# A trunk kernel's hand-overs between matmul stages: products, PSUM copies and tiles in another order

## The chip, the cores and the metric

The kernel runs on one core of one Trainium2 chip. The metric is the device time of one execution in microseconds; before the change it is 2490.99 us (median of 3 runs, 2490.53 to 2492.29).

## The reference

The input x is 256 tokens by 4096. All tensors are float32. One layer is computed, and a final RMSNorm:

```python
h = rms_norm(x, norm_gains)
z = h @ w_in             # gq gk gv gg gdec sq sk sv sg ga gb, 19472 columns
o_a = gla_mix(gq, gk, gv, log_a)             # chunked gated linear attention, 8 heads
y_a = (rms_norm(o_a, gain) * silu(gg)) @ w_gla_out         # 2048 x 4096
o_b = swa_sink_mix(sq, sk, sv, sinks)        # sliding window, 32 query heads
y_b = (o_b * silu(sg)) @ w_swa_out           # 2048 x 4096
merged = sigmoid(ga + b0) * y_a + sigmoid(gb + b1) * y_b
x = x + merged @ w_out                       # 4096 x 4096
out = rms_norm(x, final_norm_gain)
```

## The kernel before

A float32 product is made of three matmuls: each operand is split into a rounded half (`hi`, type float32r) and the rest (`lo`), and hi·hi, hi·lo and lo·hi are summed in one PSUM bank (lines 162 to 164 and 234 to 236). ScalarE (ACT) casts `hi` from a loaded weight chunk of 128x1024, VectorE (DVE) subtracts to get `lo`; `halves` does this for every chunk. SP issues the weight loads.

TensorE goes through the stages in this order: the GLA blocks (`gq gk gv gg`, by `gemm`, 192 matmuls for a block of 512 columns), `ya` (`spilled`: four pairs of blocks; the sums are copied to `ya_d` and sent to DRAM), the sliding-window blocks (`sk sv sq sg`), `yb` (as `ya`), eight pairs `ga0 gb0 ga1 ... gb3` of the merge gates, whose results are multiplied with the reloaded y and summed in `m`, and four pairs `o0` to `o3` of the last product with `mT`, the transposed m.

`pair` computes two blocks of 512 columns for both row tiles, 8 contractions j (`ya`, `yb`) or 16 (`ga`, `gb`, `o`). A plain j takes eight products, each of three matmuls, into banks 2, 3, 4 and 8. For the j in the table `SEVEN` it takes seven (a Strassen-like scheme, one product fewer) that also use banks 1, 5, 6 and 7; for this DVE forms three sums of weight chunks (`t`, `u`, `s`, lines 214 to 216), and `combine` forms the matching sums of the left factor once for a whole stage (`xca`, `xcb`, `xch`, `xcm`). The first pair of a stage takes all eight products in every j, since its `combine` is not made yet. Before the change the table begins with j = 0.

At the end of a pair `outputs` copies bank 1 with ACT (line 253) and adds the other seven on DVE (line 247). All eight banks are then in use, and the next pair's first products go to banks that must be emptied first.

At the end of a GLA or window stage the gated result is transposed by TensorE (`transpose_split`, line 288) into `oaT` or `obT`, with a cast on ACT (line 278) and a subtraction on DVE (line 279); after `gb3` sixteen such steps make `mT` from `m`. At the start `first_inputs` makes hT, the scaled input, chunk by chunk during `gq`, squares the input on ACT (line 129) and adds the squares on GpSimd (line 130). At the end the kernel adds x, squares, takes the sum and scales (lines 655 to 669).

A scheduler of the framework puts the instructions in order. Each engine takes its own in that order, one by one. `tc.high_priority` (400 for `gemm`, 120 for `pair`) lets loads, casts and subtractions slip ahead. DMAs that ACT issues (y, bias, spills) stand in ACT's queue and wait there for what they send.

## Time and profile before

| | |
|---|---|
| median of 3 runs | 2490.99 us |
| the profiled execution | 2495.09 us |
| its span, first to last instruction | 2493.4 us |
| TensorE busy | 2437.6 us, 98% |
| VectorE, ScalarE busy | 1724.6 us, 1225.4 us |
| HBM | 476.61 MB read, 12.58 MB written |

The profiled execution is 4.1 us longer than the median, and its span leaves 1.7 us of it outside. The granted TensorE clock (PEclk) is 1.00 at the full 2.4 GHz and 0.50 at 1.2 GHz; a window's number is the mean. A matmul's listed length overlaps the next one's; the pace is the distance between starts.

### The profile page before, as it was taken

Reading aid. Unit: us, or ns where it says so; the run is one execution under the profiler, and the core shown is the slowest. Engines: PE = TensorE matmul, PEld = TensorE weight load, DVE = VectorE, ACT = ScalarE, POOL = GpSimd, SP = SyncE. Lnnn points to the kernel's source line nnn. Section 1 sums busy time; section 2 is a strip of 40 time slices with the busy share of each in tenths; the row PEclk is TensorE's granted clock in tenths of the full one; section 3 lists DMA queues with packets and bytes.
Section 4 is the critical chain, followed back from the end, with each engine's and each line's share of the span. In section 5 each row is a group of like instructions: output and inputs, shape, how many; then the busy total and the mean of one; then the engine's idle time right before and its main releaser. Section 6 shows DMA issues by size and latency. Waiting matters only on the chain.

```text
span 2493.4 us, 29365 instructions
## 1 busy us (share of the span) xinstructions
PE 2437.6 (98%) x10986; PEld 1999.0 (80%) x10986; DVE 1724.6 (69%) x1929; ACT 1225.4 (49%) x1479; POOL 42.5 (2%) x52
## 2 busy tenths in 40 slices
...
GB/s 250 157 169 192 170 176 194 170 170 204 191 223 183 192 179 160 152 186 152 161 178 193 218 245 185 213 227 228 216 216 227 216 227 216 202 186 216 225 221 191
DMA packets 139024, 491.14 MB, mean 197 GB/s; under 512 B 15840, under 2 KB 16224, under 8 KB 138880
## 3 DMA queue, kind: packets, MB, share of 16 engines
...
HBM read 476.61 MB, written 12.58 MB: 196 GB/s over the span
## 4 chain that ended last, share of the span: by engine, by line
PE 89%; DVE 5%; issue 2%; DMA 2%; ACT 1%; POOL 0%; SPq 0%; ACTq 0%; POOLq 0%; DVEq 0%
PE ga_q L234 5%; PE ga_q L236 4%; PE ga_q L235 4%; PE gb_q L236 4%; PE gb_q L234 4%; PE gb_q L235 4%; PE o_q L236 4%; PE o_q L235 4%; PE o_q L234 4%; PE sg_a L163 2%; PE sg_a L162 2%; PE sq_a L164 2%; PE sq_a L163 2%; PE sq_a L162 2%; PE sg_a L164 2%; PE gg_a L164 2%
## 5 line engine op out<-in xcount | busy, mean ns | idle before, releaser
L214 DVE TENSOR_TENSOR gb_t<-gb_r,gb_s 128x1024 f32<-128x1024 f32 x24 | 29.3, 1221 | 11.0 <-DMA gb_s<-in_wgate_dram 11.0
L103 POOL TENSOR_TENSOR st<-st,mhalf 128x1 f32<-128x1 f32 x2 | 1.1, 553 | 1700.4 <-DVE st L102 1700.4
L565 ACT ACTIVATE s<-s,mx 128x128 f32<-128x128 f32 x64 | 28.4, 445 | 0.0
L214 DVE TENSOR_TENSOR o_t<-o_r,o_s 128x1024 f32<-128x1024 f32 x18 | 22.0, 1221 | 9.1 <-DMA o_s<-in_wout_dram 9.1
L130 POOL TENSOR_TENSOR ssq<-ssq,sq 128x512 f32<-128x512 f32 x15 | 26.4, 1757 | 25.3 <-ACT sq L129 24.7
L214 DVE TENSOR_TENSOR ga_t<-ga_r,ga_s 128x1024 f32<-128x1024 f32 x18 | 22.0, 1221 | 4.9 <-DMA ga_s<-in_wgate_dram 4.7
L121 DVE SCALAR_TENSOR_TENSOR hT<-xsb,gin_sb,hT 128x256 fp32r<-128x256 f32 x32 | 21.9, 733 | 4.9 <-ACT hT L120 4.9
L550 DVE SCALAR_TENSOR_TENSOR s<-s,mask 128x384 f32<-128x384 f32 x32 | 16.0, 552 | 6.0 <-PE s L549 6.0
L143 ACT CAST sg_16h<-sg_r 128x1024 fp32r<-128x1024 f32 x4 | 4.2, 1056 | 28.0 <-PE sg_a L164 28.0
L214 DVE TENSOR_TENSOR ya_t<-ya_r,ya_s 128x1024 f32<-128x1024 f32 x9 | 11.0, 1222 | 8.6 <-DMA ya_s<-in_wgla_dram 8.6
L214 DVE TENSOR_TENSOR yb_t<-yb_r,yb_s 128x1024 f32<-128x1024 f32 x9 | 11.0, 1222 | 8.4 <-DMA yb_s<-in_wswa_dram 8.4
L657 ACT ACTIVATE xt<-x 128x512 f32<-128x512 f32 x16 | 10.1, 630 | 13.7 <-DVE x L247 13.7
L216 DVE TENSOR_TENSOR gb_s<-gb_u,gb_s 128x512 f32<-128x512 f32 x24 | 16.5, 688 | 0.3
L215 DVE TENSOR_TENSOR gb_u<-gb_t,gb_r 128x512 f32<-128x512 f32 x24 | 16.5, 688 | 0.3
L473 DVE COPY oraw<-op 128x512 f32<-128x512 f32 x8 | 5.5, 692 | 15.6 <-PE op L472 15.6
L582 DVE COPY pT<-pt 128x384 f32<-128x384 f32 x16 | 8.9, 554 | 9.3 <-PE pt L579 9.3
L464 POOL TENSOR_SCALAR_AFFINE_SELECT ats<-ats 128x128 f32<-128x128 f32 x16 | 8.0, 523 | 415.4 <-DVE ats L462 415.4
L476 ACT ACTIVATE jk<-oraw 128x256 f32<-128x256 f32 x16 | 6.7, 418 | 16.9 <-DVE oraw L473 16.6
L579 PEld LDWEIGHTS pt<-ident,s 128*128 128x128 f32 x96 | 11.4, 145 | 4.4 <-ACT s L565 3.9
L120 ACT ACTIVATE hT<-xsb,gin_sb 128x256 fp32r<-128x256 f32 x32 | 14.1, 499 | 1.8 <-DMA xsb<-in_xT_dram 1.2
L579 PE MATMUL pt<-ident,s 128*128 128x128 f32 x96 | 14.9, 278 | 0.0
L288 PE MATMUL m_t<-ident,m 128*128 128x128 f32 x64 | 10.2, 302 | 3.7 <-DVE mT L279 3.7
...
## 6 DMA issues: line engine op xcount, KB each, us to landing
...
```

Of the source, the lines that this page charges most:

```text
L121: nc.vector.scalar_tensor_tensor(hT[:, kt, 1, :], xsb[:, kt, :], g, hT[:, kt, 0, :].bitcast(F32), ALU.mult, ALU.subtract)
L130: nc.gpsimd.tensor_tensor(ssq, ssq, sq, ALU.add)
L162: nc.tensor.matmul(acc[t], lh, hi[:, i, :], start=kt == 0, stop=False)
L163: nc.tensor.matmul(acc[t], lh, lo[:, i, :], start=False, stop=False)
L164: nc.tensor.matmul(acc[t], ll, hi[:, i, :], start=False, stop=kt == nkt - 1)
L214: nc.vector.tensor_tensor(ts, r1, r2[:, 0:1, :].broadcast_to([P, 2, NB]), ALU.add)
L215: nc.vector.tensor_tensor(t2[:, 0, :], ts[:, 1, :], r1[:, 0, :], ALU.add)
L234: nc.tensor.matmul(q[i], lh, hi[:, c, :], start=done[i] == 1, stop=False)
L235: nc.tensor.matmul(q[i], lh, lo[:, c, :], start=False, stop=False)
L236: nc.tensor.matmul(q[i], ll, hi[:, c, :], start=False, stop=done[i] == total[i])
L565: nc.scalar.activation(s4[:, k, cs], s4[:, k, cs], AF.Exp, bias=mx[:, k, t : t + 1], accum_out=sm[:, k, t : t + 1],)
L579: nc.tensor.transpose(tp[:, m * P : (m + 1) * P], s4[:, k, m * P : (m + 1) * P], ident)
```

## The change

The diff is below; in words:

- **Products.** `SEVEN` becomes (1, 4, 6, 9, 11, 13) for 16 contractions and (1, 3, 5) for 8, so every pair begins with eight products into banks 2, 4, 3 and 8. The first pairs of `ya`, `yb` and the gates now use seven products from contraction 4 (`ya0`, `yb0`: j = 5) or 8 (`ga0`: j = 9, 11, 13) on; `first_pair` spreads `combine` over their first contractions. `o0` keeps eight throughout.
- **End of a pair.** The last contraction's eight products are sorted by bank (2, 4, 3, 8), so that the sums end one after the other. ACT copies these four and bank 1; DVE makes eight additions, five of them with a PSUM operand.
- **Last gate pair.** `gb3` and `o3` keep the additions of before; sums of `gb3` are followed at once by transposes (`merged`), the rest of the gate comes behind, and the last four transposes and the `combine` of `mT` stand inside `o0`.
- **Tiles.** `oraw`, `ss`, `gt`, `gng_sb`, `on` and `sg` move to pools of their own (`glo`, `slo`), and the staging tiles of mixed stages are laid out in a fixed order (`mixed_staging`), so the first loads and casts of `ya` and `yb` reuse other memory than before.
- **Squares.** Written in the loop of `gk` instead of that of `gq`.
- **End of the kernel.** x is loaded in one piece per pair and added in `outputs`; seven of eight partial sums of squares are reduced early; the last gain is applied with the final scaling; the output goes in six pieces per row tile instead of four.

```diff
-SEVEN = {16: (0, 3, 5, 8, 10, 13), 8: (0, 2, 5)}
+SEVEN = {16: (1, 4, 6, 9, 11, 13), 8: (1, 3, 5)}
...
+        def squares(k0, n):
             xr = xsb[:, k0 : k0 + n, :]
-            if k0 < KW:
-                nc.scalar.activation(ssq[:, k0 : k0 + n, :], xr, AF.Square)
+            if k0 == 0:
+                nc.scalar.activation(ssq, xr, AF.Square)
                 return
             sq = gp.tile([P, KW, S], F32, tag="sq", name=f"sq{k0}", bufs=2)
             nc.scalar.activation(sq, xr, AF.Square)
             nc.gpsimd.tensor_tensor(ssq, ssq, sq, ALU.add)
 
-        return before
+        return before, squares
...
+    def mixed_staging():
+
+        cur["n"], cur["r"] = STM, 6
+        for tag, n, dt, bufs in (("hi", 2, F32R, STM), ("raw", 2, F32, 6), ("t2", 1, F32, 1), ("t13", 2, F32, 1), ("lo", 2, F32R, STM)):
+            cur["hl"].tile([P, n, NB], dt, tag=tag, name=f"first_{tag}", bufs=bufs)
+
+    def combine(lhs, xc, js, name, at=None):
 
 
         for c, j in enumerate(js):
+            if at is not None and at != c:
+                continue
...
-        sev = SEVEN[npr] if xc is not None else ()
+    def pair(name, lhs, w, npr, xc=None, before=None, last=False, since=0):
+
+        sev = [j for j in SEVEN[npr] if j >= since] if xc is not None else ()
...
+            if not last and j == npr - 1:
+                work.sort(key=lambda x: (2, 4, 3, 8).index(x[0]))
             if last and j == npr - 1:
-                work.sort(key=lambda x: x[0] in (4, 8))
+                work.sort(key=lambda x: {4: 1, 8: 2}.get(x[0], 0))
...
-    def outputs(q, d, name, pool):
-
+    def outputs(q, d, name, pool, extra=None, late=None):
+
+
+        quarters = ((0, 0, 2), (1, 0, 4), (0, 1, 3), (1, 1, 8))
         if 1 in q:
             v = pool.tile([P, NB], F32, tag="yr", name=f"{name}_v", bufs=2)
+        if 1 in q and late is None:
+            for t, i, b in quarters:
+                nc.scalar.copy(d[t][i], q[b])
+            nc.scalar.copy(v, q[1])
+            add(d[0][0], q[1], d[0][0])
+            add(v, q[6], v)
+            add(d[0][1], q[5], d[0][1])
+            add(d[1][1], q[5], d[1][1])
+            add(d[0][1], d[0][1], v, ALU.subtract)
+            add(v, q[7], v)
+            add(d[1][0], d[1][0], v)
+            add(d[1][1], d[1][1], v, ALU.subtract)
+        elif 1 in q:
             nc.scalar.copy(d[0][0], q[1])
             add(v, q[6], d[0][0])
             add(d[0][1], q[5], v, ALU.subtract)
             add(d[1][0], q[7], v)
             add(d[1][1], q[5], d[1][0], ALU.subtract)
-        for t, i, b in ((0, 0, 2), (0, 1, 3), (1, 0, 4), (1, 1, 8)):
-            if 1 in q:
+        for do in (late or ())[:1]:
+            do()
+        for t, i, b in quarters:
+            if 1 not in q:
+                if extra is not None:
+                    add(d[t][i], q[b], extra[t][i])
+                else:
+                    nc.scalar.copy(d[t][i], q[b])
+                continue
+            if extra is not None:
+                add(d[t][i], d[t][i], extra[t][i])
+            if late is not None:
                 add(d[t][i], q[b], d[t][i])
-            else:
-                nc.scalar.copy(d[t][i], q[b])
+        for do in (late or ())[1:]:
+            do()
+
+    def first_pair(lhs, xc, npr, name, order, since, n):
+
+        if n > 0:
+            return {}
+
+        def before(j):
+            if 1 <= j <= len(order):
+                combine(lhs, xc, SEVEN[npr], name, at=order[j - 1])
+
+        return {"before": before, "since": since}
 
     def spilled(name, lhs, w, dst, xc, pool):
 
         for n in range(NP2):
-            q = pair(f"{name}{n}", lhs, w[n], OKT // 2, xc=None if n == 0 else xc)
+            q = pair(f"{name}{n}", lhs, w[n], OKT // 2, xc=xc, **first_pair(lhs, xc, OKT // 2, name, (2, 0, 1), 4, n))
...
+    with phase("hl0") as cur["hl"], phase("gla") as gp, phase("glo") as glo:
         cur["n"], cur["r"] = STG, 4
         ssq = gp.tile([P, KW, S], F32, name="ssq")
-        q0 = zblock("gq", 0, before=first_inputs(gp, ssq), chunks=RAMP)
-        k0 = zblock("gk", 0)
+        load, squares = first_inputs(gp, ssq)
+        q0 = zblock("gq", 0, before=load, chunks=RAMP)
+        k0 = zblock("gk", 0, before=squares)
...
-                gt = gp.tile([P, NT, 2 * DV], F32, tag="gt", name=f"gt{pi}")
+                gt = glo.tile([P, NT, 2 * DV], F32, tag="gt", name=f"gt{pi}")
...
-        cur["n"], cur["r"] = STM, 6
+        mixed_staging()
...
+    mTs = []
+
+    def merged(j0, j1):
+
+        if j0 == 0:
+            mTs.append(big.tile([P, KT, 2, S], F32R, tag="hT", name="mT"))
+        for j in range(j0, j1):
+            transpose_split(mTs[0], 2 * j, m[:, :, 2 * j * P : 2 * (j + 1) * P], 2, f"m{j}")
+
     for n in range(NP2):
         for w, (kind, y_d) in enumerate((("ga", ya_d), ("gb", yb_d))):
             cs = [slice((2 * n + i) * NB, (2 * n + i + 1) * NB) for i in range(2)]
             bt = ep.tile([P, 2, NB], F32, tag="bt", name=f"bt{w}{n}")
             nc.scalar.dma_start(bt, bgates[w, 2 * n * NB : 2 * (n + 1) * NB].partition_broadcast(P).rearrange("p (i c) -> p i c", i=2))
-            q = pair(f"{kind}{n}", hT, wgate[w * NP2 + n], KT // 2, xc=None if n + w == 0 else xch)
-            if n + w == 0:
-                combine(hT, xch, SEVEN[KT // 2], "h")
+            q = pair(
+                f"{kind}{n}", hT, wgate[w * NP2 + n], KT // 2, xc=xch,
+                **first_pair(hT, xch, KT // 2, "h", (3, 4, 5, 0, 1, 2), 8, n + w),
+            )
             d = ep.tile([P, NT, 2, NB], F32, tag="ev", name=f"{kind}_d{n}")
-            outputs(q, [[d[:, t, i, :] for i in range(2)] for t in range(NT)], f"{kind}{n}", ep)
+            mt = [lambda: merged(0, 2), lambda: merged(2, 3 * KT // 8)] if w == 1 and n == NP2 - 1 else None
...
-    st = ep.tile([P, NT, NBLK + 1], F32, tag="ev", name="st")
-    for j in range(KT // 2):
-        transpose_split(mT, 2 * j, m[:, :, 2 * j * P : 2 * (j + 1) * P], 2, f"m{j}")
+    st = const.tile([P, KT], F32, tag="kt", name="st")[:, : NT * (NBLK + 1)].rearrange("p (t n) -> p t n", t=NT)
     x2 = big.tile([P, NT, DM], F32, tag="oT", name="x2")
+    sf = [st[:, t, NBLK:] for t in range(NT)]
+    sums = lambda j: (
+        combine(mT, xcm, SEVEN[KT // 2], "m", at=j - 9) if j >= 9
+        else transpose_split(mT, 2 * (j + 10), m[:, :, 2 * (j + 10) * P : 2 * (j + 11) * P], 2, f"m{j + 10}") if 2 <= j < 6
+        else None
+    )
...
+        q = pair(f"o{n}", mT, wout[n], KT // 2, xc=None if n == 0 else xcm, last=last, before=sums if n == 0 else None)
...
-        outputs(q, [[x2[:, t, cs[i]] for i in range(2)] for t in range(NT)], f"o{n}", ep)
         gf = ep.tile([P, 2, NB], F32, tag="bt", name=f"gf{n}")
         nc.scalar.dma_start(gf, gfin[2 * n * NB : 2 * (n + 1) * NB].partition_broadcast(P).rearrange("p (i c) -> p i c", i=2))
+        xt = ep.tile([P, NT, 2, NB], F32, tag="ev", name=f"xt{n}")
+        nc.scalar.dma_start(xt, x[:, 2 * n * NB : 2 * (n + 1) * NB].rearrange("(t p) (i c) -> p t i c", p=P, i=2))
+        outputs(
+            q, [[x2[:, t, cs[i]] for i in range(2)] for t in range(NT)], f"o{n}", ep,
+            extra=[[xt[:, t, i, :] for i in range(2)] for t in range(NT)], late=[] if last else None,
+        )
         for t in range(NT):
             for i in range(2):
                 xq = x2[:, t, cs[i]]
-                xt = ep.tile([P, NB], F32, tag="yr", name=f"xt{n}{t}{i}", bufs=2)
-                nc.scalar.dma_start(xt, x[t * P : (t + 1) * P, cs[i]])
-                add(xq, xq, xt)
-                nc.scalar.activation(xt, xq, AF.Square, accum_out=st[:, t, 2 * n + i : 2 * n + i + 1])
-                add(xq, xq, gf[:, i, :], ALU.mult)
+                nc.scalar.activation(xt[:, t, i, :], xq, AF.Square, accum_out=st[:, t, 2 * n + i : 2 * n + i + 1])
+                if not last or i == 0:
+                    add(xq, xq, gf[:, i, :], ALU.mult)
+                if last and i == 0:
+
+                    nc.vector.tensor_reduce(sf[t], st[:, t, : NBLK - 1], AX.X, ALU.add)
+                    nc.vector.tensor_scalar(sf[t], sf[t], 1.0 / DM, EPS, ALU.mult, ALU.add)
     for t in range(NT):
-        sf = st[:, t, NBLK:]
-        nc.vector.tensor_reduce(sf, st[:, t, :NBLK], AX.X, ALU.add)
-        rms_scale(sf, sf, DM)
-        for c in range(4):
-            os = slice(c * 1024, (c + 1) * 1024)
-            if c % 2 == 0:
-                nc.vector.tensor_scalar(x2[:, t, os], x2[:, t, os], sf, None, ALU.mult)
+        nc.vector.tensor_scalar(sf[t], st[:, t, NBLK - 1 : NBLK], 1.0 / DM, sf[t], ALU.mult, ALU.add)
+        nc.gpsimd.tensor_tensor(sf[t], sf[t], mhalf[:, 0:1], ALU.pow)
+        at = 0
+        for c, w in enumerate((512, 512, 1024, 1024, 512, 512)):
+            os = slice(at, at + w)
+            at += w
+            if at == DM:
+                nc.vector.scalar_tensor_tensor(x2[:, t, os], x2[:, t, os], sf[t], gf[:, 1, :], ALU.mult, ALU.mult)
+            elif c % 2 == 0:
+                nc.vector.tensor_scalar(x2[:, t, os], x2[:, t, os], sf[t], None, ALU.mult)
             else:
-                nc.scalar.activation(x2[:, t, os], x2[:, t, os], AF.Copy, scale=sf)
+                nc.scalar.activation(x2[:, t, os], x2[:, t, os], AF.Copy, scale=sf[t])
             nc.sync.dma_start(out[t * P : (t + 1) * P, os], x2[:, t, os])
```

Three places show how the instruction order moves. The first is ACT between the pairs `ga1` and `gb1`: `ga_d1` is the tile of ga1's results, `q2` to `q8` are banks, `r`, `s`, `t`, `u` are weight chunks and their sums, and `h` marks a cast. Before:

```order
L143 CAST ga1_s15h_12597<-ga1_s15_12591 128x1024
L143 CAST gb1_t0h_12675<-gb1_t0_12670 128x1024
L143 CAST gb1_u0h_12679<-gb1_u0_12671 128x512
L626 DMA yga100_12636<-ya_d_63 128x512
L143 CAST gb1_r0h_12683<-gb1_r0_12666 128x1024
L626 DMA yga101_12641<-ya_d_63 128x512
L143 CAST gb1_s0h_12687<-gb1_s0_12668 128x1024
L143 CAST gb1_r1h_12716<-gb1_r1_12712 128x1024
L143 CAST gb1_s1h_12720<-gb1_s1_12714 128x1024
```

After:

```order
L145 CAST gb1_r0h_12811<-gb1_r0_12807 128x1024
L145 CAST gb1_s0h_12815<-gb1_s0_12809 128x1024
L145 CAST gb1_t1h_12852<-gb1_t1_12847 128x1024
L269 COPY ga_d1_12762<-ga1_q2_12122 128x512
L269 COPY ga_d1_12762<-ga1_q4_12124 128x512
L686 ACTIVATE ga_d1_12762<-ga_d1_12762 128x512
L269 COPY ga_d1_12762<-ga1_q3_12123 128x512
L145 CAST gb1_u1h_12856<-gb1_u1_12848 128x512
L684 DMA yga101_12782<-ya_d_63 128x512
L145 CAST gb1_r1h_12860<-gb1_r1_12843 128x1024
L269 COPY ga_d1_12762<-ga1_q8_12125 128x512
L145 CAST gb1_s1h_12864<-gb1_s1_12845 128x1024
```

The four copies and a sigmoid (line 686) now stand between the casts for the first two contractions of `gb1`; the reloads of y come behind.

The second is ACT between `ya3`, the last pair of `ya`, and `sk0`, the first window block; the DMA rows send the sums to DRAM. Before:

```order
L143 CAST ya3_r7h_5546<-ya3_r7_5542 128x1024
L253 COPY ya_d3_5578<-ya3_q1_5252 128x512
L143 CAST ya3_s7h_5550<-ya3_s7_5544 128x1024
L271 DMA ya_d_63<-ya_d3_5578 128x1024 x2
L143 CAST sk0_0h_5616<-sk0_r0_5614 128x1024
```

After:

```order
L270 COPY ya3_v_5619<-ya3_q1_5292 128x512
L145 CAST ya3_s7h_5590<-ya3_s7_5584 128x1024
L269 COPY ya_d3_5618<-ya3_q2_5296 128x512
L269 COPY ya_d3_5618<-ya3_q4_5298 128x512
L269 COPY ya_d3_5618<-ya3_q3_5297 128x512
L269 COPY ya_d3_5618<-ya3_q8_5299 128x512
L319 DMA ya_d_63<-ya_d3_5618 128x1024 x2
L145 CAST sk0_0h_5663<-sk0_r0_5661 128x1024
```

The four copies, and the two DMAs that wait for them and for DVE's additions, stand ahead of the first cast of `sk0`.

The third is DVE between `gb3` and `o0`: `gb_d3` holds gb3's results, `m` the merged rows, the rows of `mT` are the lower halves of transposed pieces `m0`, `m1` and so on, and those with `o0` prepare weight chunks. Before:

```order
L247 TENSOR_TENSOR gb_d3_16018<-gb3_q4_15380,gb_d3_16018 128x512
L247 TENSOR_TENSOR gb_d3_16018<-gb3_q8_15381,gb_d3_16018 128x512
L627 SCALAR_TENSOR_TENSOR gb_d3_16018<-gb_d3_16018,rstd_82,bt13_15372 128x512 x3
L247 TENSOR_TENSOR gb_d3_16018<-gb_d3_16018,ygb300_16029 128x512
L247 TENSOR_TENSOR gb_d3_16018<-gb_d3_16018,ygb301_16035 128x512
L247 TENSOR_TENSOR m_10636<-m_10636,gb_d3_16018 128x512 x2
L627 SCALAR_TENSOR_TENSOR gb_d3_16018<-gb_d3_16018,rstd_82,bt13_15372 128x512
L279 TENSOR_TENSOR mT_16053<-m0_t0_16056,mT_16053 128x2x256
L247 TENSOR_TENSOR gb_d3_16018<-gb_d3_16018,ygb310_16041 128x512
L247 TENSOR_TENSOR gb_d3_16018<-gb_d3_16018,ygb311_16047 128x512
L247 TENSOR_TENSOR m_10636<-m_10636,gb_d3_16018 128x512 x2
L279 TENSOR_TENSOR mT_16053<-m1_t0_16063,mT_16053 128x2x256
```

After:

```order
L259 TENSOR_TENSOR gb_d3_16175<-gb3_q3_15536,gb_d3_16175 128x512
L685 SCALAR_TENSOR_TENSOR gb_d3_16175<-gb_d3_16175,rstd_82,bt13_15529 128x512
L259 TENSOR_TENSOR gb_d3_16175<-gb3_q8_15538,gb_d3_16175 128x512
L146 TENSOR_TENSOR o0_s1l_16347<-o0_s1_16340,o0_s1h_16346 128x1024
L325 TENSOR_TENSOR mT_16182<-m0_t0_16183,mT_16182 128x2x256
L325 TENSOR_TENSOR mT_16182<-m1_t0_16190,mT_16182 128x2x256
L325 TENSOR_TENSOR mT_16182<-m2_t0_16201,mT_16182 128x2x256
L325 TENSOR_TENSOR mT_16182<-m3_t0_16208,mT_16182 128x2x256
L146 TENSOR_TENSOR o0_r2l_16386<-o0_r2_16381,o0_r2h_16385 128x1024
L325 TENSOR_TENSOR mT_16182<-m4_t0_16215,mT_16182 128x2x256
```

The lower halves of `m0` and the following pieces now come right behind gb3's last sum; the multiplications with y and the additions into `m` come after `m11`.

## Rows read from the trace of the kernel before

**Rows 1.** The page, part 1: busy us of each engine.

```profile
PE 2437.6 (98%) x10986; PEld 1999.0 (80%) x10986; DVE 1724.6 (69%) x1929; ACT 1225.4 (49%) x1479; POOL 42.5 (2%) x52
```

**Rows 2.** Windows of stages: busy us of engines, granted clock (1.00 is full).

```profile
core 0: us, PE busy (x) PEld busy (x) DVE busy (x) ACT busy (x) POOL busy (x), PEclk, DMA share, GB/s
5.40:61.50 56.10, 51.43 (x192) 39.72 (x193) 46.85 (x50) 38.75 (x66) 26.36 (x15) 0.94 0.75 260
597.10:775.50 178.40, 171.93 (x741) 139.85 (x741) 131.84 (x144) 85.13 (x91) 0.00 (x0) 0.99 0.61 204
...
1630.80:1713.80 83.00, 83.00 (x368) 68.61 (x367) 74.53 (x83) 45.27 (x49) 0.00 (x0) 1.00 0.69 222
2128.80:2150.60 21.80, 18.11 (x101) 15.01 (x100) 20.91 (x32) 13.26 (x22) 0.00 (x0) 0.84 0.58 181
2479.30:2493.40 14.10, 0.00 (x0) 0.00 (x0) 5.71 (x11) 4.67 (x8) 0.56 (x1) 0.62 0.75 299
```

**Rows 3.** Waits of PE: us in total, times, longest.

```profile
PE yb_q L234 <- DVE yb_d L247: 4.1, 2, 2.5
PE yb_q L234 <- ACT yb_r0h L143: 3.9, 1, 3.9
PE ya_q L234 <- ACT ya_r0h L143: 3.9, 1, 3.9
PE m_t L288 <- DVE mT L279: 3.7, 1, 3.7
PE ya_q L234 <- DVE ya_d L247: 3.4, 2, 2.0
...
PE sk_a L162 <- ACT sk_0h L143: 2.3, 1, 2.3
```

**Rows 4.** Windows around four hand-overs between stages or pairs.

```profile
589.10:602.10 13.00, 7.55 (x22) 5.02 (x22) 12.23 (x24) 7.09 (x9) 0.00 (x0) 0.61 0.68 229
686.00:696.00 10.00, 7.58 (x32) 5.68 (x32) 9.12 (x12) 3.53 (x4) 0.00 (x0) 1.00 0.75 252
1275.00:1289.00 14.00, 7.52 (x22) 5.47 (x23) 12.00 (x22) 7.92 (x11) 0.00 (x0) 0.63 0.54 169
1372.00:1382.00 10.00, 7.15 (x30) 5.12 (x29) 9.79 (x13) 3.05 (x5) 0.00 (x0) 1.00 0.72 241
```

**Rows 5.** Groups of DVE by form in a ga pair; count, busy, mean ns.

```profile
L247 DVE TENSOR_TENSOR ga_d<-ga_q,ga_d 128x512 f32<-128x512 f32 x3 | 2.0, 688 | 0.0
...
L144 DVE TENSOR_TENSOR ga_r1l<-ga_r,ga_r1h 128x1024 fp32r<-128x1024 f32 x1 | 1.2, 1226 | 0.1
```

**Rows 6.** Groups of ACT by form, 1700 to 1712 us.

```profile
L143 ACT CAST ga_s15h<-ga_s 128x1024 fp32r<-128x1024 f32 x1 | 1.1, 1054 | 0.0
...
L253 ACT COPY ga_d<-ga_q 128x512 f32<-128x512 f32 x1 | 0.6, 577 | 0.0
```

**Rows 7.** Timeline of ACT, GLA to ya: start, length, idle before.

```profile
592.49 1.23 ACT L278 CAST oaT<-oa_t 128x512 fp32r<-128x512 f32 x2 [2.22 <-PE oa_t L288]
...
595.93 1.04 ACT L143 CAST ya_r0h<-ya_r 128x1024 fp32r<-128x1024 f32 x1
```

**Rows 8.** Timeline of ACT, ya to sk.

```profile
773.31 1.01 ACTq L271 DMA_DIRECT2D ya_d<-ya_d  x2
774.41 1.04 ACT L143 CAST sk_0h<-sk_r 128x1024 fp32r<-128x1024 f32 x1 [11.99 <-DVE ya_d L247]
```

**Rows 9.** Timeline of DVE, gb to o.

```profile
2135.66 0.69 DVE L279 TENSOR_TENSOR mT<-m_t,mT 128x512 fp32r<-128x512 f32 x1
...
2138.85 1.88 DVE L279 TENSOR_TENSOR mT<-m_t,mT 128x512 fp32r<-128x512 f32 x3
```

**Rows 10.** Timeline of DVE, end of the kernel.

```profile
2479.59 1.28 DVE L247 TENSOR_TENSOR x<-o_q,x 128x512 f32<-128x512 f32 x2
...
2484.49 1.42 DVE L666 TENSOR_SCALAR x<-x,st 128x1024 f32<-128x1024 f32 x2 [0.67 <-POOL st L103]
```

**Rows 11.** DMA, 2470 to 2494 us: GB/s in 40 slices of 0.6 us.

```profile
GB/s 0 0 0 0 109 300 27 0 0 0 0 34 188 341 270 41 218 410 403 403 403 410 410 396 403 41 89 396 403 410 389 403 416 396 403 191 14 0 0 0
```

29 lines of the change are left out of this document (11 added, 18 removed).

## The prediction

> **What bounds the kernel now.** The page's first part comes first: TensorE (PE) is busy for 2437.6 us of the span [rows 1], so only what PE does slowly, or waits for, can be gained. The table of windows gives its pace [rows 2]: a gate pair takes 83.0 us, PE busy for all of them, and has 366 matmuls (the row lists two of its neighbours' as well), so 0.227 us each. In that pair VectorE (DVE) works 74.5 us and ScalarE (ACT) 45.3: neither is waited for, and work that moves from one to the other there gains nothing by itself. The time that PE loses lies at the hand-overs, and PE's list of waits names them [rows 3]: 4.1 and 3.4 us in two waits each between pairs of `yb` and of `ya`, 3.9 at the start of either, 3.7 among the transposes before `o0`, 2.3 at `sk`. The windows around them [rows 4] add what the list doesn't hold: the granted clock. It is 1.00 at the pair boundaries, though PE waits up to 2.5 us there, and 0.61 and 0.63 around the starts of `ya` and `yb`, where PE has little to do for some 4 us and more. In a window of 21.8 us at 0.84 [rows 2], gb to o, (1 - 0.84) x 21.8 = 3.5 us go to the clock. Before the first matmul and after the last one PE can't be busy; the end is 14.1 us [rows 2].
>
> **The change part by part.** I write E for the moment when a pair's last matmul has been issued; a consumer of its bank starts about 0.2 us later.
>
> *Products.* `ya0` and `yb0` have one product less, `ga0` three: 5 x 3 matmuls x 0.227 = **3.4 us**, all on PE's own path. The DVE sums that this costs fall into pairs where DVE has room (they have no `t`, `u`, `s` sums for most contractions). Bounds 2 to 3.4.
>
> *Boundaries between pairs of ya and of yb.* The order of before has PE's first products of the next pair go to banks 5, 7, 6 and 1, which DVE empties by additions that stand among subtractions of 1.23 us each [rows 5]. In the window 686 to 696 us there are 32 matmuls, 7.3 us of work, so 2.7 us are lost, and in the one at 1372 30, so 3.2 [rows 4]: 0.7 more than the longest wait of each [rows 3], because a second short one follows. Four such boundaries lose 3.4 + 4.1 + 4 x 0.7 = 10.3 us. After the change PE needs banks 2, 4, 3 and 8, whose sums end at E - 4.1, E - 2.7, E - 1.4 and E; ACT copies each in 0.58 us [rows 6]. The last copy stands behind a cast of 1.05 us that waits for E itself: E + 0.2 + 1.05 + 0.58 = E + 1.8, and PE is at bank 8 after nine matmuls, E + 2.04. Tight, but in time; next come the sums for `t` of j = 3, which wait for a load. I keep a third of a microsecond at each of four: **8.9 us**. Bounds 5 to 10.3.
>
> *Boundaries that lose nothing now* (gates, `o`: ten). ACT has the four copies, and in the gates a sigmoid between them that waits for DVE. Worked through in the same way, the copy of bank 8 ends near E + 2.3 and PE needs it at E + 2.5, since in the order eleven matmuls stand ahead of it. The additions that stay on DVE are as many as before and as long. **0 us**; bounds -32 to 0, the lower one from 3.2 us at each, the loss in [rows 4] of a boundary that is late.
> A copy of 128x512 out of PSUM takes ACT 0.577 us and an addition takes DVE 0.688 [rows 5, 6], and DVE is the fuller of the two.
> The Trainium skill speaks against these copies: "ScalarE: Activation LUTs", section "Rules for kernel authors", tells to give additions and the like to VectorE and not to ScalarE. By the rule the change hands work to the engine that does it worse, and the sum would be that of the rival in which ACT is late (2498.9); the rows above don't agree with it here, and I go by them.
>
> *GLA to ya, and sg to yb.* At `ya` ACT waits for the transposes, casts `oaT` at 592.49, then sits behind a cast of a combined left factor that waits for DVE, and only at 595.93 begins the cast of the first weight chunk, `ya_r0h` [rows 7]. In the new order that cast comes right after the first of the two `oaT` casts. One DVE addition (0.69, [rows 5]) slips ahead of the gating before, so: 592.49 + 0.7 + 0.62 + 1.04 = 594.9 instead of 597.0, **2.1 us**. Bounds 0 to 3.9, the wait in [rows 3]. At `yb` the first three casts are ahead of those of `obT`; PE starts with the contractions whose left factors are there already and doesn't stand before the transposes: the wait of 3.9 us [rows 3] goes, **3.9 us**. Bounds 1 to 6; the clock still falls in both.
>
> *ya to sk* gets worse. Now two spill DMAs sit in ACT's queue until DVE's last additions, and the first cast of `sk` follows at 774.41 [rows 8]. After the change they wait for the copy of bank 8 (E + 0.8) and the four additions behind it, 4 x 0.62 = 2.5; then about 0.45 for the second issue, and the cast, 1.04: E + 4.8. Before, PE waits 2.3 us [rows 3] and is at E + 2.4. **-2.4 us**; bounds -5 (a lower clock for longer) to 0. What is behind the DMAs on ACT is only the casts of `sk`, and PE waits for just these.
>
> *gb to o.* The excess is the wait of 3.7 [rows 3] plus 3.5 of clock: 7.2 us. DVE sets it: m0's lower half runs at 2135.66 and the next three only from 2138.85 [rows 9], since multiplications and additions of the gate stand ahead, and the transposes of the fifth piece wait for a bank. In the new order the halves come behind the last sum and one 1.23 subtraction: E + 0.2 + 0.6 + 1.1 = E + 1.9, a half every 0.62 us from then on. PE has sixteen transposes and four matmuls first, until about E + 2.7. Waits of about 0.2 us remain at some banks, 1 to 1.5 us together, with the wait then too short for a fall of the clock: **5.5 us**. Bounds 2 to 7.2. The displaced gate work lands beside `o0`, which has plain contractions only, and four pieces of mT are due only at contraction 12.
> If the clock falls there all the same, 3.5 of the 5.5 are not gained: 2470.4.
> [...]
>
> *The end.* Before, PE's last matmul is followed by two sums, two additions of x, squares, a reduction, a power on GpSimd and the last scaling, which begins at 2484.49, 5.2 us after the last matmul at 2479.3 [rows 2, 10]. After it: one sum (to E + 0.95), a square (0.63 and the read, E + 1.8), one small DVE step, the power (0.56, [rows 2]): E + 2.9. That is 2.3 sooner. But the output is 4.19 MB and the DMAs move it at about 403 GB/s [rows 11], in two bursts with a gap between: the first row tile leaves some 1 us earlier now, and 10.4 us of transfer from E - 0.5 end at E + 9.9, then 1.9 for what comes after the last data now: E + 11.8 against 14.1. **2.2 us**; bounds 0 to 4.
>
> *The start.* The fifteen GpSimd additions (26.4 us) lie within `gq`, whose 192 matmuls take 56.1 us instead of 43.6 [rows 2]. The code moves the squares, but in the built order they still stand among the casts of `gq`: hidden or not, they stay. One cast comes earlier, **0.5 us**; bounds -3 to 5.
>
> Sum: 3.4 + 8.9 + 0 + 2.1 + 3.9 - 2.4 + 5.5 + 2.2 + 0.5 = 24.1 us. The profiled execution took 2495.09 us, so it would take 2471.0; it lies 4.1 over the median of the runs, 2490.99, and the forecast for that is **2466.9 us**.
>
> **The rivals.**
> - *Hand-overs only move.* Each term at `ya`, `yb`'s start, `o0` and the start of the kernel rests on one order being kept to within a microsecond; where another operand is late instead, the 2.1 + 3.9 + 5.5 + 0.5 are gone: 2466.9 + 12.0 = 2478.9. For it: DVE is at 20.9 of 21.8 us in gb to o [rows 2] and all its items stay. Against: the waits in [rows 3] name the very casts and halves that come earlier.
> - *All of it comes.* The bounds at their better ends (3.4 + 10.3 + 3.9 + 6 + 0 + 7.2 + 4 + 5 = 39.8): 2451.2. Squares that leave `gq` after all would be part of that.
> - *ACT is late at ten boundaries.* One mechanism: the sigmoid between the copies waits for DVE, the copy of bank 8 behind it comes after PE needs it, and so does every cast behind that. Slack by my count is 0.2 us, and one more 1.05 cast ahead breaks it. At 3.2 us each: 32 us, 2498.9, slower. It decides from 2.4 us at each (24.1 / 10). Against: ACT has 37.7 of 83.0 us free [rows 2], and in `o` no sigmoid stands there.
>
> **How the numbers follow.** Forecast 0.56 (own range 2459 to 2475; 0.15 of it for the clock that falls at `o0` all the same, 2470.4), hand-overs only move 0.24, all of it 0.13, ACT late 0.05, other 0.02. The range to 2452 takes in nearly all of the better case, and to 2483 the worse one on the same side. A measurement of this kernel tells about 0.2%, 5 us, from no change. Faster than 2486: 0.56 + 0.13 + most of the 0.24, 0.92; same 0.04; slower 0.04.
>
> **What would show it.** In the profile after: 15 matmuls fewer; no waits of PE on `ya_d`, `yb_d`; `ya_q` waiting for a cast for about 2 us less; the wait at `sk` at 4 to 5 us; no stretch of low clock at `o0`; an end of 12 us. The forecast is wrong if PE gets waits on ACT copies (line 269) inside the gates, or if `m_t` still waits for `mT` for over 2 us.

## The result and the profile after

The changed kernel takes 2510.81 us (median of 4 runs, 2510.06 to 2513.05), the one before 2490.81 in the same comparison: a ratio of 1.0079 (95% interval 1.0063 to 1.0095). It is 20 us slower, where 24 us faster was forecast. The spans of the profiled executions are 2509.1 and 2493.4 us. The profile after lies at its median, the one before 4.1 us over its own, so the two profiles differ by 15.8 us and not by 20.

Part 1 of the page of the kernel after answers to [rows 1]: the fifteen matmuls are gone, and PE is busy for 2 us more all the same.

```profile
PE 2439.7 (97%) x10971; PEld 1991.4 (79%) x10971; DVE 1758.4 (70%) x1982; ACT 1260.0 (50%) x1543; POOL 41.1 (2%) x52
```

The starts of the first matmuls of each stage, read from PE's records in both traces, divide these 15.8 us. In the table the last column is what the stage gained (+) or lost.

| stretch | before, us | after, us | gained |
|---|---|---|---|
| start of the span to `gk` | 61.53 | 58.72 | +2.8 |
| `gk` to `ya` | 535.49 | 532.49 | +3.0 |
| `ya` to `sk` | 178.49 | 183.75 | -5.3 |
| `sk` to `yb` | 507.92 | 502.40 | +5.5 |
| `yb` to `ga0` | 177.20 | 180.00 | -2.8 |
| eight gate pairs | 668.15 | 690.80 | -22.6 |
| transposes of m, then `o` to its last matmul | 350.51 | 348.00 | +2.5 |
| after the last matmul | 14.08 | 12.96 | +1.1 |

(In the row of `sk` to `yb`, `yb` starts some matmuls earlier than before, ahead of its transposes; with the row under it the two gain 2.7.)

PE's waits after, beside [rows 3] (us in total, times, longest):

```profile
PE gb_q L246 <- ACT ga_d L269: 8.2, 8, 1.6
PE ga_q L246 <- ACT gb_d L269: 6.4, 6, 1.4
...
PE sk_a L164 <- ACT sk_0h L145: 4.8, 1, 4.8
PE ya_q L246 <- DVE ya_v L259: 3.3, 3, 1.4
PE yb_q L246 <- DVE yb_v L259: 3.2, 3, 1.4
...
PE ya_q L247 <- DVE ya_r4l L146: 2.3, 3, 0.8
```

The two waits of 3.9 us at the starts of `ya` and `yb` have fallen to 1.3 and 1.2, and the 3.7 at `m_t` is gone, much as forecast. In their place stand waits that before didn't exist, on ScalarE's copies (line 269) inside the gates, fourteen of them with 14.6 us in all, which is the sign that the forecast had named for its being wrong.

Windows after, beside [rows 2, 4] and with their columns: the start, `ya`, a gate pair (`ga1`), ten microseconds near its beginning, the boundary behind it, gb to o, the end.

```profile
5.40:58.70 53.30, 47.54 (x192) 36.88 (x193) 48.71 (x50) 38.73 (x65) 24.95 (x15) 1.00 0.77 270
591.20:775.00 183.80, 172.85 (x739) 139.65 (x739) 141.55 (x161) 94.67 (x109) 1.21 (x4) 0.98 0.61 202
1629.00:1716.30 87.30, 85.22 (x368) 69.77 (x368) 74.82 (x83) 47.31 (x53) 0.00 (x0) 0.98 0.66 212
1632.00:1642.00 10.00, 9.17 (x33) 7.10 (x34) 8.88 (x13) 5.56 (x7) 0.00 (x0) 0.83 0.43 133
1716.00:1726.00 10.00, 7.98 (x34) 5.96 (x34) 9.23 (x14) 5.27 (x7) 0.00 (x0) 1.00 0.35 111
2148.20:2170.00 21.80, 21.61 (x121) 18.03 (x120) 21.02 (x30) 14.79 (x23) 0.00 (x0) 1.00 0.52 167
2496.20:2509.10 12.90, 0.00 (x0) 0.00 (x0) 4.88 (x12) 3.26 (x5) 0.56 (x1) 0.70 0.84 326
```

Gb to o holds 121 matmuls, short transposes among them, where it held 101, and its clock is full now. The gate pair has the same 368, and takes 87.3 us instead of 83.0, though DVE has as much to do in it as before (74.8 us against 74.5) and ACT, with nearly half of its time still free, only 2 us more (47.3 against 45.3): what changed is who waits for whom. The granted clock of 0.83 in ten of its microseconds costs 0.17 x 10 = 1.7 us of the 4.3; the window of 1889 to 1899 us, behind another boundary, has 0.83 as well.

The timeline of ScalarE at the boundary of `ga1` and `gb1`, whose first matmul starts at 1716.29, shows it (start, length, idle before and what ended it):

```profile
1713.89 1.06 ACT L269 COPY ga_d<-ga_q 128x512 f32<-128x512 f32 x2
1717.84 0.63 ACT L686 ACTIVATE ga_d<-ga_d 128x512 f32<-128x512 f32 x1 [2.89 <-DVE ga_d L685]
1718.37 0.57 ACT L269 COPY ga_d<-ga_q 128x512 f32<-128x512 f32 x1
1718.84 0.62 ACT L145 CAST gb_u1h<-gb_u 128x512 fp32r<-128x512 f32 x1
1719.22 0.33 ACTq L684 DMA_DIRECT2D yga<-ya_d  x1
1719.67 1.05 ACT L145 CAST gb_r1h<-gb_r 128x1024 fp32r<-128x1024 f32 x1 [0.20 <-ACT gb_u1h L145]
1720.63 0.57 ACT L269 COPY ga_d<-ga_q 128x512 f32<-128x512 f32 x1
```

ScalarE has copied banks 2 and 4, stands idle for 2.89 us at the sigmoid (the ACTIVATE), and only then copies banks 3 and 8, though both have long been ready. The copy of bank 8 ends 4.9 us after the pair's first matmul; the forecast had E + 2.3. PE pays twice:

```profile
1718.99 0.50 PE L246 MATMUL gb_q<-gb_r0h,hT 128*128 128x512 f32 x1 [1.18 <-ACT ga_d L269]
1721.25 0.50 PE L246 MATMUL gb_q<-gb_r0h,hT 128*128 128x512 f32 x1 [0.84 <-ACT ga_d L269]
```

DVE at the same place is why the sigmoid is late:

```profile
1711.59 1.23 DVE L224 TENSOR_TENSOR gb_t<-gb_r,gb_s 128x1024 f32<-128x1024 f32 x1 [3.07 <-DMA gb_s<-in_wgate_dram]
...
1715.20 1.22 DVE L146 TENSOR_TENSOR gb_t1l<-gb_t,gb_t1h 128x1024 fp32r<-128x1024 f32 x1
1716.34 0.68 DVE L259 TENSOR_TENSOR ga_d<-ga_q,ga_d 128x512 f32<-128x512 f32 x1
1717.05 0.75 DVE L685 SCALAR_TENSOR_TENSOR ga_d<-ga_d,rstd,bt 128x512 f32<-128x512 f32 x1
1718.50 0.69 DVE L259 TENSOR_TENSOR m<-ga_d,yga 128x512 f32<-128x512 f32 x1 [0.69 <-ACT ga_d L686]
```

It waits 3.07 us for the second weight chunk of contraction 1, now the first with seven products. Four more instructions that prepare weights stand behind the sum, and only then come the addition and the scaling that the sigmoid needs. The groups of this sum (line 214 before, 224 after; the last figure is the idle time before it) say that it happens everywhere. Before:

```profile
L214 DVE TENSOR_TENSOR ga_t<-ga_r,ga_s 128x1024 f32<-128x1024 f32 x18 | 22.0, 1221 | 4.9 <-DMA ga_s<-in_wgate_dram 4.7
...
L214 DVE TENSOR_TENSOR ya_t<-ya_r,ya_s 128x1024 f32<-128x1024 f32 x9 | 11.0, 1222 | 8.6 <-DMA ya_s<-in_wgla_dram 8.6
```

After:

```profile
L224 DVE TENSOR_TENSOR ga_t<-ga_r,ga_s 128x1024 f32<-128x1024 f32 x21 | 25.7, 1224 | 33.0 <-DMA ga_s<-in_wgate_dram 33.0
...
L224 DVE TENSOR_TENSOR ya_t<-ya_r,ya_s 128x1024 f32<-128x1024 f32 x10 | 12.3, 1226 | 20.1 <-DMA ya_s<-in_wgla_dram 20.1
```

### The profile page after: what moved, and what is told of

Same layout as the page of the kernel before. It is cut to its first block, busy times and chain, and to the rows that moved or that the text cites. A ratio compares the mean times of both kernels' runs of the same rounds, so it can differ in the third digit from the quotient of the medians.

```text
span 2509.1 us, 29357 instructions
## 1 busy us (share of the span) xinstructions
PE 2439.7 (97%) x10971; PEld 1991.4 (79%) x10971; DVE 1758.4 (70%) x1982; ACT 1260.0 (50%) x1543; POOL 41.1 (2%) x52
## 5 line engine op out<-in xcount | busy, mean ns | idle before, releaser
L121 DVE SCALAR_TENSOR_TENSOR hT<-xsb,gin_sb,hT 128x256 fp32r<-128x256 f32 x32 | 27.2, 898 | 3.7 <-ACT hT L120 3.7
L224 DVE TENSOR_TENSOR ya_t<-ya_r,ya_s 128x1024 f32<-128x1024 f32 x10 | 12.3, 1226 | 20.1 <-DMA ya_s<-in_wgla_dram 20.1
L686 ACT ACTIVATE ga_d<-ga_d 128x512 f32<-128x512 f32 x16 | 9.6, 627 | 12.5 <-DVE ga_d L685 12.5
L686 ACT ACTIVATE gb_d<-gb_d 128x512 f32<-128x512 f32 x16 | 9.7, 630 | 11.9 <-DVE gb_d L685 11.8
L246 PE MATMUL gb_q<-gb_r0h,hT 128*128 128x512 f32 x16 | 7.3, 454 | 8.2 <-ACT ga_d L269 8.2
L269 ACT COPY ya_d<-ya_q 128x512 f32<-128x512 f32 x16 | 9.3, 585 | 11.9 <-PE ya_q L248 11.8
```

Source lines behind the costliest of these rows:

```text
L121: nc.vector.scalar_tensor_tensor(hT[:, kt, 1, :], xsb[:, kt, :], g, hT[:, kt, 0, :].bitcast(F32), ALU.mult, ALU.subtract)
L224: nc.vector.tensor_tensor(ts, r1, r2[:, 0:1, :].broadcast_to([P, 2, NB]), ALU.add)
L246: nc.tensor.matmul(q[i], lh, hi[:, c, :], start=done[i] == 1, stop=False)
L686: nc.scalar.activation(dq, dq, AF.Sigmoid)
```

## The experiments

Two readings of this offered themselves. SIGMOID: an instruction that waits for DVE stands between ScalarE's copies. LATE LOAD: the first sum of a pair waits for its load, and all of DVE's work behind it is late, whoever empties the banks. In the table of gates "eight pairs" is read as above, first matmul of `ga0` to first transpose of m; ratios are to the kernel before, run beside each.

### Pairs taken apart: table, copies

Each run starts from the kernel after unless another is named. Run 1 takes the old contractions, run 3 lets DVE empty the banks, run 4 does both and takes the old order of the last products too.

```
run 1:  SEVEN = {16: (0, 3, 5, 8, 10, 13), 8: (0, 2, 5)}
run 3:  outputs(..., late=[])             # in ya, yb, the gates and o
run 4:  both, and without
        -  if not last and j == npr - 1: work.sort(... (2, 4, 3, 8) ...)
```

> Contractions 0, 3, 5, 8, 10, 13 (0, 2, 5 in ya and yb) take the seven products again, as before the change; all else of the change stays, ScalarE's copies and the sigmoid between them too. A pair of the gates took 83.0 us before and 86.4 us after (mean of eight), 184 us from ya to sk. Theory LATE LOAD (the first seven-product contraction is now the second of a pair, DVE waits 2.5 to 3.1 us for a chunk of its weights, and all that stands behind it in DVE's queue is late): DVE's t sum runs some 8 us earlier than the end of a pair again, the gate pairs go back to 83.0 to 83.8, ya to sk to about 180; total 2479 to 2487. Theory SIGMOID (a sigmoid that waits for DVE stands between ScalarE's copies of the banks, whatever the table): the gates stay at 85.5 or more, only ya and yb gain; 2500 to 2512.

> After the change, with the four sums taken out of PSUM by DVE as before the change, not by ScalarE; new table and the last contraction's new order stay. Theory SIGMOID: ScalarE has no bank to empty and its sigmoid holds nothing up, gate pairs about 83 to 84, total 2488 to 2496. Theory LATE LOAD: the additions that empty banks now stand in DVE's own queue behind the sum that waits for its load, four of 0.69 us each more, so a boundary loses as much as after or more: gate pairs 86 to 88, total 2508 to 2525.

> The pairs as before the change (old contractions with seven products, old order of the last products, DVE takes the sums), with the rest of the change: start, left factors and their casts earlier at ya, sk and yb, the transposes of m as soon as its halves are there, the end row tile by row tile. By either theory the gates return to 83.0 us a pair, ya and yb to the boundary waits of before, and what the rest of the change gained stays: 2.8 at the start, 3.0 from GLA to ya, about 3 from sg to yb, 5.3 from gb to o, 1.1 at the end; ya to sk is as before. Total 2490.8 - 15 = 2475.6; 2472 to 2482. If one of these gains was only wait moved out of the pairs, 2480 to 2488.

Measured: run 1 2518.74 us, ratio 1.0105 (1.0088 to 1.0121), eight pairs 688.6 us, `ya` to `sk` 192.0; run 3 2505.74, 1.0049 (1.0034 to 1.0064), eight pairs 690.2; run 4 2479.55, 0.9945 (0.9930 to 0.9960), eight pairs 666.1. Run 1 misses both totals; run 3 lies between its two, with the gates (86.3 us a pair) where LATE LOAD has them. LATE LOAD as it was put there, as a cause by itself, falls with run 1: with the sum early again the gates lose as much. But SIGMOID's figure for the gates (85.5 or more a pair; 86.1) is met for another reason. PE's waits of run 1:

```profile
PE ya_q L247 <- DVE ya_s3l L146: 5.9, 3, 2.1
...
PE ga_q L246 <- DVE gb_v L259: 5.1, 3, 1.8
...
PE gb_q L246 <- DVE ga_v L259: 4.5, 4, 1.3
```

and of run 3:

```profile
PE gb_q L246 <- DVE ga_d L259: 6.3, 4, 2.1
PE ga_q L246 <- DVE gb_d L259: 6.1, 3, 2.6
```

The old contractions need the banks 5, 7, 6 and 1 first, and with ScalarE's copies DVE's additions that empty these come last (`v` takes in banks 6 and 7); the new contractions need 2, 4, 3 and 8 first, and without the copies DVE empties these last. Table and copies fit only together, and half of the change costs the gates as much as the whole. Run 4 shows what the rest of the change is worth: 13.6 us, where 15 was expected.

Run 1 tells one thing more. At each of its seven boundaries between gate pairs DVE's sum has its load, ScalarE stands at the sigmoid for only 0.47 us, and the copy of bank 8 ends 2.0 us after the pair's first matmul (here of `gb1`, at 1723.03); the load of y comes behind that copy here:

```profile
1721.56 0.63 ACT L686 ACTIVATE ga_d<-ga_d 128x512 f32<-128x512 f32 x1 [0.47 <-DVE ga_d L685]
...
1724.50 0.57 ACT L269 COPY ga_d<-ga_q 128x512 f32<-128x512 f32 x1
```

### The gate by row tiles

```
-  nc.vector.scalar_tensor_tensor(dq, dq, rs(t), bt[:, i, :], ALU.mult, ALU.add)   # four of 512
-  nc.scalar.activation(dq, dq, AF.Sigmoid)
+  nc.vector.scalar_tensor_tensor(d[:, t], d[:, t], rs(t), bt, ALU.mult, ALU.add)  # two of 1024
+  nc.scalar.activation(d[:, t], d[:, t], AF.Sigmoid)
```

> After the change, with the gate's scaling and sigmoid done once per row tile over 1024 elements instead of once per 512: the first sigmoid can then stand only behind the copies of banks 2, 4 and 3, and the second behind that of bank 8. The table stays new. Theory SIGMOID: PE's waits of about 1.4 us for bank 3 and 1.0 us for bank 8 at each boundary of the gates go, gate pairs at 83.5 to 84.5, total 2490 to 2496. Theory LATE LOAD: DVE is still late; PE gets bank 3 and 8 in time, but waits instead for the casts and sums of the first seven-product contraction; gate pairs 85 to 86.5, total 2502 to 2512. ya and yb stay as after in both.

Measured: 2493.10 us, 1.0001 (0.9991 to 1.0010); eight pairs 673.3 us, 17.5 less; `ya` and `yb` 182.9 and 178.2. As SIGMOID has it. Of the 24.7 us by which the gates after stand above run 4 (690.8 against 666.1, the same matmuls), 7.2 stay. ScalarE in this run, around the first matmul of `gb1` at 1708.70:

```profile
1705.95 1.06 ACT L269 COPY ga_d<-ga_q 128x512 f32<-128x512 f32 x2
1707.54 0.59 ACT L269 COPY ga_d<-ga_q 128x512 f32<-128x512 f32 x1 [0.52 <-PE ga_q L248]
...
1709.90 0.58 ACT L269 COPY ga_d<-ga_q 128x512 f32<-128x512 f32 x1
...
1714.44 1.06 ACT L682 ACTIVATE ga_d<-ga_d 128x1024 f32<-128x1024 f32 x1 [1.70 <-DVE ga_d L681]
```

The copy of bank 8 ends 1.8 us after that matmul, not 4.9. DVE's sum still waits 2.7 us for its load in this boundary, and PE isn't stopped by it.

### Which instruction holds the copies

The run above moves more than the sigmoid: the load of the second piece of y, which ScalarE issues and which waits for DVE's product of the first, moves behind the copies with it. So the sigmoid was left out (run 12), the loads of y given to GpSimd (run 13), and both (run 14), each in the kernel after the change. Runs 12 and 14 leave out a part of the computation: they answer a question and are no faster versions.

```
run 12:  -  nc.scalar.activation(dq, dq, AF.Sigmoid)
run 13:  -  nc.scalar.dma_start(y, ...)      +  nc.gpsimd.dma_start(y, ...)
run 14:  both
```

> The change itself, with the sixteen pieces of 512 of the gate left unsquashed: the sigmoid is left out in ga and gb (part of the computation is missing), all else stays, table 1, 3, 5 too. Of ScalarE's queue at a boundary of the gates only the activation between the copies of banks 4 and 3 goes; the load of the second piece of y still stands ahead of the copy of bank 8 and waits for DVE's product of the first. Theory SIGMOID: the copies of 3 and 8 come on time, gate pairs from 690.8 us in all to 670 to 677 (second run: 673.3), span 2488 to 2495. If the load of y holds bank 8 up just as well, only the wait for bank 3 goes: 680 to 684. If the second run gained by having fewer and longer operations: 687 to 691. ya and yb stay (183.8 and 180.0).

> The change itself, with the loads of y in the gates issued by GpSimd, not by ScalarE; the sigmoid stays between the copies of banks 4 and 3. Theory EITHER (each instruction that waits for DVE's chain holds the copies behind it, so that taking one away leaves the other): the waits for bank 3 (1.4 us) and most of that for bank 8 stay, gate pairs 685 to 691 us in all, span 2503 to 2510. Theory Y LOAD (the sigmoid's wait is too short to matter by itself): 670 to 677, span 2489 to 2496.

> The twelfth run (the gate's sigmoid left out) with the loads of y issued by GpSimd: nothing that waits for DVE's chain is left between ScalarE's four copies, pieces of 512 and the new table stay. Theory EITHER and theory Y LOAD: the copy of bank 8 comes about 1.8 us after the pair's last matmul as in the second run, not 4.2; gate pairs 670 to 677, span 2489 to 2496. If the second run gained by fewer and longer operations, or if DVE's lateness behind the late load is enough by itself: 685 or more, span over 2503.

| kernel | between the copies | bank 8 copied, after first matmul of `gb1` | eight pairs | ratio (95%) |
|---|---|---|---|---|
| after | sigmoid, load of y | 1721.20 - 1716.29 = 4.9 | 690.8 | 1.0079 (1.0063 to 1.0095) |
| run 12 | load of y | 1720.14 - 1715.97 = 4.2 | 692.6 | 1.0090 (1.0061 to 1.0119) |
| run 13 | sigmoid | 1716.79 - 1713.18 = 3.6 | 684.9 | 1.0068 (1.0051 to 1.0085) |
| run 14 | neither | 1712.05 - 1710.27 = 1.8 | 672.4 | 1.0018 (1.0009 to 1.0028) |

ScalarE in run 12: the copies of 2, 4 and 3 are done, and the queue stops at the load.

```profile
1714.81 0.59 ACT L269 COPY ga_d<-ga_q 128x512 f32<-128x512 f32 x1 [0.76 <-PE ga_q L248]
1717.67 0.33 ACTq L684 DMA_DIRECT2D yga<-ya_d  x1
1718.09 0.62 ACT L145 CAST gb_u1h<-gb_u 128x512 fp32r<-128x512 f32 x1 [2.69 <-DVE m L259]
1718.61 1.04 ACT L145 CAST gb_r1h<-gb_r 128x1024 fp32r<-128x1024 f32 x1
1719.56 0.58 ACT L269 COPY ga_d<-ga_q 128x512 f32<-128x512 f32 x1
```

In run 13 the sigmoid alone stands there, and the copy of bank 8 is late all the same:

```profile
1713.73 0.63 ACT L686 ACTIVATE ga_d<-ga_d 128x512 f32<-128x512 f32 x1 [2.48 <-DVE ga_d L685]
...
1716.20 0.59 ACT L269 COPY ga_d<-ga_q 128x512 f32<-128x512 f32 x1
```

In run 14:

```profile
1709.11 0.59 ACT L269 COPY ga_d<-ga_q 128x512 f32<-128x512 f32 x1 [0.77 <-PE ga_q L248]
1709.83 0.62 ACT L145 CAST gb_u1h<-gb_u 128x512 fp32r<-128x512 f32 x1
1710.51 1.05 ACT L145 CAST gb_r1h<-gb_r 128x1024 fp32r<-128x1024 f32 x1
1711.47 0.58 ACT L269 COPY ga_d<-ga_q 128x512 f32<-128x512 f32 x1
```

SIGMOID was too narrow and run 12 refutes it: without the sigmoid nothing is gained (its 692.6 include three falls of the clock behind waits of 2.1 to 3.1 us). Two instructions stand between the copies and wait on one chain of DVE, and taking away one leaves the other: run 13 recovers 5.9 us, run 12 none, and without either the gates recover 18.4. Run 14 keeps the pieces of 512, so it isn't fewer operations that helped run 2, and keeps the new table, so of the 24.7 us DVE's lateness can cost the gates at most 6.3 while no copy waits for it.

Where an instruction does stand there, the copy of bank 8 keeps step with DVE's first sum. At the seven boundaries of the kernel after and the seven of run 9 (below) the sum waits 2.7 to 4.3 us for its load, and the copy ends 9.6 us after the sum's start at every one, 4.5 to 6.2 us after the pair's first matmul. In run 12 it is 9.4 us and in run 13 9.3 at every one. In run 14 the copy ends 1.8 us after the first matmul at each, whether the sum starts 4.9 or 6.4 us before that. So the late load sets how late the copies are, and the instructions between them pass it on. Without the one (run 1, though with another table) or the other (run 14) the copies come in time.

### ya and yb: spills, or loads

There no sigmoid stands between the copies, but the spills of `ya_d` and `yb_d` are in ScalarE's queue and wait for DVE's last additions. Runs 5 to 7 start from run 2.

```
run 5:  -  nc.scalar.dma_start(dst[t]..., d[:, t]...)   +  nc.gpsimd.dma_start(...)
run 6:  in ya alone, tag "raw": 6 buffers -> 8
run 7:  SEVEN[8]: (1, 3, 5) -> (1, 4, 6)
```

> The gate by rows as in the second run, and the two spills of each pair of ya and yb issued by GpSimd, not by ScalarE, whose casts then no longer stand behind a wait for DVE's last additions (3.3 and 3.1 us idle at the first boundary of ya). Base: ya to sk 182.9 us, yb 178.2, gap before sk 5.2, span 2489.9. Theory SPILL (the boundaries of ya and yb lose 2.7 us each because ScalarE's queue is held by the spills): each boundary loses about 1 us, gap before sk 2 us; ya to sk 174 to 177, yb 173 to 175; span 2478 to 2482. Theory DVE LATE (DVE runs without a pause there and empties bank 7 late, because it had waited for a load in front): only the gap before sk shrinks, by 2.5 to 4 us; ya to sk 179 to 180.5, yb 177.5 to 178.5; span 2485 to 2488.

> The gate by rows as in the second run, and in ya alone eight raw buffers for weights instead of six, so that a load is issued one contraction earlier; yb and the gates keep six (eight don't fit there) and serve as the control. Base: ya to sk 182.9 us, yb 178.2. Theory DVE LATE by its loads: DVE no longer waits 2.6 us for the second chunk of the contraction with seven products, PE's waits for bank 7 (1.4 us) and for r4l (0.8 us) at three boundaries go; ya to sk 175.5 to 178, yb unchanged. Theory SPILL: ya stays at 181.5 to 183. If it is DVE's amount of work alone, the same.

> The gate by rows as in the second run, and in ya and yb contractions 1, 4 and 6 with seven products instead of 1, 3 and 5: the second of them comes one contraction later, further behind the boundary, and the first pair has two of them instead of one, so one product (3 matmuls, 0.7 us) less in each of ya0 and yb0. Theory DVE LATE (too many sums of DVE right behind a boundary): the second wait of each boundary (r4l, 0.8 us and 0.1 to 0.6 for s3l) goes, the first (bank 7, 1.4 us) becomes smaller, since t3 no longer stands ahead of the additions; ya to sk 177.5 to 180, yb 173.5 to 175.5. Theory SPILL: only the product is gained, ya to sk 182, yb 177.5.

Measured: run 5 2493.57 us, 1.0002 (0.9993 to 1.0011), `ya` to `sk` 180.6 and `yb` 178.5; run 6 2484.03, 0.9971 (0.9962 to 0.9981), 174.4 and 180.1; run 7 2472.15, 0.9928 (0.9910 to 0.9947), 173.4 and 169.2. So not the spills: only the stretch before `sk` gained, and less than the first reading expected there (the first matmul waits 1.6 us, and a second one 2.1 for DVE). The loads are the cause, shown twice. Run 6 carries its own control, the group of the same sum in `yb`:

```profile
L224 DVE TENSOR_TENSOR yb_t<-yb_r,yb_s 128x1024 f32<-128x1024 f32 x10 | 12.2, 1225 | 21.4 <-DMA yb_s<-in_wswa_dram 21.4
L224 DVE TENSOR_TENSOR ya_t<-ya_r,ya_s 128x1024 f32<-128x1024 f32 x10 | 12.2, 1220 | 0.1
```

With eight buffers DVE's 20.1 us of waiting are 0.1, and `ya` is 8.5 us shorter; in `yb`, with six, the wait is as long as ever (21.4) and the stage gained nothing (180.1 against 178.2 in run 2). Run 7 gained more than expected (9.4 and 9.0 us, 0.7 of each for the product, against 3 to 5): a sum one contraction later took all of PE's waits at these boundaries away, not half of them.

### Separate causes, and versions that beat both

Run 8 is run 4 with the spills of run 5. Run 9 is the change with (1, 4, 6) alone. Run 10 has the new pairs, with (1, 4, 6), in `ya` and `yb`, and the old ones in the gates and `o`; in run 11 DVE empties the last pair of `ya` besides.

```
run 10:  SEVEN = {16: (0, 3, 5, 8, 10, 13), 8: (1, 4, 6)}
         work.sort(... (2, 4, 3, 8) ...) if npr == 8; late=[] in gates and o
run 11:  + late=[] if name == "ya" and n == NP2 - 1
```

> The old pairs of the fourth run (2477.0 us span, ya to sk 181.2, yb 179.7), with the spills issued by GpSimd. The wait of 2.2 us before sk goes to 0.5 or less, since the cast of the first chunk has only to wait for its load. At the boundaries of ya and yb PE waits for DVE there (banks 5, 7, 6, 1). Theory SPILL: DVE is late because casts are; waits of 5.8 and 4.1 us fall to under half; ya to sk 176 to 177.5, yb 177 to 178; span 2469 to 2471.5. Theory DVE LATE: only the wait before sk; ya to sk 179 to 180, yb as it was; span 2474.5 to 2476.

> The change itself (gate in pieces of 512 with the sigmoid between the copies) with contractions 1, 4, 6 instead of 1, 3, 5 in ya and yb and nothing else. If the two causes (sigmoid between the copies in the gates; DVE behind a late load in ya and yb) are separate, ya and yb gain what they gained in the seventh run against the second, 9.4 + 9.0 us, and the eight gate pairs stay at 690.8 us (within 4): total 2490 to 2495. If the late load was a cause in the gates too, carried over from yb, the gates fall to 685 or less: under 2488.

> New pairs with contractions 1, 4, 6 in ya and yb, where no sigmoid stands between the copies, and the old pairs (old contractions, old order of the last products, DVE takes the sums) in the gates and o; all else of the change stays. By stages: ya to sk 173.4 and yb 169.2 as in the seventh run, gates 666.1 and o 342.3 as in the fourth: span 2468.6 - 4.6 - 4.9 = 2459.1, median about 2462.6 (2459 to 2466). If the two kinds of pair disturb each other where they meet (yb to ga0), 1 to 3 us more.

> The same, and ya's last pair alone is emptied by DVE, so that before sk ScalarE's queue has no copies and additions to wait for. The wait before sk falls from 4.8 us to 2.2 as in the fourth run: 2.4 us less than the run beside it, median about 2460. If ScalarE's queue is held by the spills there in either way, no difference.

Measured: run 8 2476.68 us, 0.9936 (0.9922 to 0.9951), its boundaries wait for DVE as in run 4 (5.4 and 4.6 us) and only `ya` to `sk` and `yb` gain, 1.6 and 1.4, of which the start gives 2.2 back (`gk` at 60.99 us, with a granted clock of 0.94 in `gq`). Run 9 2495.72, 1.0017 (1.0004 to 1.0031): `ya` and `yb` gain 9.4 and 12.4, and the gates stay bad, at 697.9 (7 more than expected; one pair of 90.8 us is most of that), so the late loads of `ya` and `yb` aren't what the gates lose by; what the two stages gained is their own. Run 10 2461.50, 0.9882 (0.9867 to 0.9896), where 2462.6 was expected. Run 11 2457.35, 0.9864 (0.9850 to 0.9879): 34.7 us under the kernel before, run beside it, and 53 under the change. It is 4.2 us less than run 10, 2.5 of it from `ya` to `sk`, where 2.4 was expected. Its windows of `ya`, `yb` and a gate pair:

```profile
592.74:763.90 171.16, 168.94 (x735) 139.25 (x735) 145.15 (x166) 94.30 (x107) 1.20 (x4) 0.99 0.66 216
1265.08:1434.26 169.18, 169.18 (x742) 139.86 (x742) 149.62 (x175) 99.11 (x114) 0.00 (x0) 0.99 0.67 223
1602.36:1685.36 83.00, 83.00 (x368) 68.61 (x366) 74.55 (x83) 45.27 (x49) 0.00 (x0) 1.00 0.68 222
```

## Why the prediction was wrong

The step that failed is the count of what the boundaries between pairs lose. Put beside the forecast's terms, the two profiles say:

- **Boundaries that lose nothing now**, 0 us: this step failed, and decided. The eight gate pairs lost 22.6 us though they have nine matmuls less (2.0 us), so 24.7, and `o1` to `o3` lost 3.4, 28.1 in all; the term's own bounds, -32 to 0, took that in, the forecast's range didn't. In the gates 14.6 us are PE's waits for ScalarE's copies and 3.4 the two falls of the clock behind them. The forecast counted the sigmoid between the copies and gave the copy of bank 8 a slack of 0.2 us (E + 2.3 against E + 2.5); it ended 4.7 to 5.3 us after the pair's first matmul, which starts at E. Two things were missing from the count. DVE's first sum waits 2.9 to 3.5 us for a load, and all that the sigmoid needs stands behind it. And a load of y stands between the copies as well: the order printed with the change has it there (`yga101`, ahead of the copy of bank 8), while the sentence under that order says that the reloads of y come behind. Runs 2 and 14 bring 17.5 and 18.4 us back. In `o` no sigmoid stands between the copies, which the forecast held against this loss, but a square does (line 719), and it waits for DVE in the same way, 2.1 us each at the starts of `o2` and `o3`. Run 4, in which ACT copies no banks there, has the loss back (342.3 us for the four pairs against 345.9).
- **Boundaries between pairs of ya and of yb**, 8.9 us gained: failed, of the wrong sign, 5.8 us lost. The text named the danger ("next come the sums for `t` of j = 3, which wait for a load") and priced it at a third of a microsecond. In `ya` and `yb` three boundaries each lost some 2 us in waits for bank 7 and `r4l`; before, two each did. Run 7 shows that the gain was there: with the sum a contraction later 9.4 + 9.0 us come back.
- **Products**, 3.4 us: right as a count, 15 matmuls less, and they lie in the stages below. But with 0.7 us saved in each of `ya0` and `yb0` came the third boundary: the pairs behind them, `ya1` and `yb1`, took 41.5 us each before, 44.4 and 43.9 after, and 45.6 and 43.6 in run 4, with the old pairs. The likely reason is that `ya0` and `yb0` now fill all eight banks, where plain products filled four; that is argued from the code, and no run changes it alone. In runs 7, 10 and 11 these pairs take 41.5 again, with the seven products left in.
- **ya to sk**, -2.4: right. The wait went from 2.3 us [rows 3] to 4.8; run 11 takes it back with DVE emptying the pair (2.2).
- **GLA to ya**, 2.1: 3.0; the wait for `ya_r0h` fell from 3.9 us [rows 3] to 1.3. **sg to yb**, 3.9: its wait fell to 1.2, and from the start of `sk` to the second pair of `yb` 5.2 us are gained, 0.7 of them for the product, so 4.5.
- **gb to o**, 5.5: 5.9, from the first transpose of m to the start of `o1` (100.8 us before, 94.9 after). The clock is at 1.00 there, and the case in which it falls is refuted.
- **The end**, 2.2: 1.1. **The start**, 0.5: 2.8, all of it inside `gq`, and not shown to be the change's doing. The granted clock of `gq` is 0.94 in the profile before [rows 2] and 1.00 after. Among the runs with the same start as after, `gk` begins at 58.2 to 58.7 us where that clock is 1.00, at 58.8 to 60.2 where it is 0.97, and at 61.0 in run 8 with 0.94, close to the 61.5 before. Why the clock falls there in one execution and not in another stays open.
- Summed up, the boundaries came out 28.1 and 14.7 us worse than forecast and the rest 2.9 better: 39.9 us, which is 24.1 + 15.8.
- The forecast gave the rival *ACT is late at ten boundaries* 5 in 100 and 2498.9 us. It named the place and the price (3.2 us each; the seven boundaries between gate pairs lost 24.7 / 7 = 3.5 each, the three of `o` 1.1 each), and was below the result because it left the gains of `ya` and `yb` standing. Its chance came from ScalarE's free time, 37.7 of 83.0 us, and that says nothing of when an instruction that waits lets the next one pass.
- The rule of the Trainium skill ("ScalarE: Activation LUTs", "Rules for kernel authors") that additions belong on VectorE pointed to the outcome that came about, but not by its reason: each copy took 0.57 us as before, and with DVE in ScalarE's place (run 3) the gates lost the same. Run 7 keeps the copies and beats the kernel before.

Left open: whether the gates, with the new table and the sigmoid where it is, would lose nothing if the load came in time. Since the copy ends 9.6 us after the sum's start, a sum 3 us earlier would by that have bank 8 copied about 1.9 us after the first matmul, in time for PE; this is an estimate from the boundaries above, and no run has such a load.
